# First steps reordered and four weight sums moved to GpSimd, in a one-layer hybrid encoder kernel

## The chip, the cores and the metric

One Trainium2 chip, one core. The metric is device time of the whole kernel in microseconds (us), median over runs. A profile of one execution goes with it: TensorE (PE, with its weight loads PEld), VectorE (DVE), ScalarE (ACT), GpSimd (POOL) and SyncE (SP), which here issues the DMAs.

## The reference

One encoder layer on x, 4096 tokens by 1024 channels, float32. Before everything stands an RMS norm; then one input projection, whose outputs are the attention's q, k, v, a gate g_a, the pooling branch's input u_p and its gate g_p.

```python
h = rmsnorm(x, pre_norm_g[l])
proj = jnp.einsum('bsd,de->bse', h, w_in[l])
q, k, v, g_a, u_p, g_p = jnp.split(proj, splits, axis=-1)
...
a = banded_attention(q, k, v, rel_bias, attn_sink[l]) * jax.nn.silu(g_a)
p = multiscale_pool(u_p, pool_w[l], pool_scale[l]) * jax.nn.silu(g_p)
mixed = jnp.einsum('bse,ed->bsd', jnp.concatenate([a, p], axis=-1), w_out[l])
x = x + rmsnorm(mixed, post_norm_g[l])
```

`rmsnorm` multiplies by the reciprocal root of the mean square and by a gain. Attention looks 128 tokens to each side, with a relative-position bias and a sink logit. `multiscale_pool` takes centred means over 2, 4, 8 and 16 tokens minus the token, maps each channel group by `pool_w` and scales it.

## The kernel before, in words

**Numbers.** A float32 operand is carried as two float16 parts, high and low; a product of two operands is three matmuls (high by high, low by high, high by low). Every operand is first scaled by a power of two that comes from a norm: `scale_pow` and `scale_of` reduce a sum of squares, turn its exponent round with shifts, and write the factor.

**Stages.** A first stage projects the three 512-channel groups called GP (the pooling gate, g_p), GA (the attention gate, g_a) and UU (pooling input times `pool_w`; the kernel multiplies these two weights first, `u_prod`). Tokens come in eight chunks of 512 (m = 0 to 7), each split in halves u = 0, 1 of 256. Each chunk of x has a channel dimension cut in pieces c = 0 to 3 (two 128-channel blocks each). Chunk 0 uses plain 2 by 2 blocks of weights (A11, A12, A21, A22) in `plain`; chunks 1 to 7 use a scheme with fewer products (`quad`) that needs sums of weight blocks, S1 to S4. These sums are made by `sum_weights`: four additions of 128x1024 float32 (`tt`, line 307), each followed by a split into high (`w_high`, ACT, line 606) and low (`w_low`, DVE, line 310). A second stage, with an order written out by hand, makes attention, the output product and the final norm.

**Order.** All of the first stage is given as steps: `do(engine, cost, key, function, reads, writes)`. `Steps.run` is a small planner: at each moment it takes, on the engine that is free first, the ready step with the lowest key, adds the stated cost, and 0.2 for a hand-over to another step. The order so found is the order in which each engine's instructions are issued. So a step's key and stated cost decide its place in the queue of its engine, and an engine that waits at an instruction holds up all that stand behind it. Where a step's key is smaller than that of others that are ready, it goes first; where nothing else is ready, a step far from due is taken.

**The first 30 us.** SP issues the loads by key: the four pieces of x for half 0 (key -9), the gain and an identity matrix, two weight tiles of GP (-8), a small table (-4.5), the other two tiles of GP (-4), x for half 1 (-3.5), two token blocks for the sums of squares of half 1 (-2.3), `pool_w` (9), four tiles `w_uT` for UU (9.5 to 9.8), four tiles of GA (10 to 10.3). PE runs dummy matmuls (`turn_over`) at three places. `first_square` (ACT), `first_add`, `first_fold` (DVE), `first_sum` (PE), `first_eps` (DVE) and `first_root` (POOL) make the reciprocal root of half 0; `spread` (PE) spreads it over the partitions (tile bc). Beside it `gain_most`, `gain_spread` and `gain_scale` make the scale of the gain (tiles gs, gsc, gh). `norm_half` (two instructions on DVE, line 310) multiplies x by gain and root; `b_high` (ACT, line 495) and `b_low` (DVE, line 307) split it. For the weights, `w_square` (ACT), `w_norm` (PE, tiles n2ga for the first two tiles, n2gb for the other two), `w_scale` (DVE), `w_high` and `w_low` give the operands. `row_prod` and `row_keep` are a small product for the attention's bias table. `plain(GP, M0)` then starts the real matmuls (line 689, tile plain), in steps of six matmuls: one block of weights by one piece c.

**Around 64 to 125 us.** DVE prepares chunk 1 (`norm`, `t_sums`, `b_low`, `t_low`), makes S1 to S4 of UU, and starts the pooling of chunk 0 (`pool_tile` on DVE, `pool_gate` on POOL). POOL also makes the reciprocal root of each chunk (`root`). In `quad` the results of UU go into one buffer, ubuf, which the pooling must have left first (a copy, line 908).

Of the kernel before, what the change touches and what calls it, by code (L numbers as in the profile page):

```python
# [8 lines left out]
F32 = mybir.dt.float32  # L9
# [16 lines left out]
NH = 8  # L26
# [108 lines left out]
def hybrid_layer(ctx: ExitStack, tc, io, out):  # L135
# [75 lines left out]
    with ExitStack() as actx:  # L211
# [139 lines left out]
        def row_prod():  # L351
            row_t["p"] = psa.tile([NH, 512], F32, name="fp", tag="n20")
            nc.tensor.matmul(row_t["p"], row_t["b"], row_t["o"], start=True, stop=True)
# [40 lines left out]
        def gain_scale():  # L394
            m2 = comm.tile([P, 1], F32, name="m2", tag="m2")
            V.tensor_reduce(out=m2, in_=bc.pop("g"), axis=mybir.AxisListType.X, op=ALU.max)
            scale_of(gs, m2, 1e-30, H_SCALE)
            t_scalar(V, gsc, g_pre, gs, ALU.mult)
            t_scalar(V, gh, gs, 1.0 / H_SCALE, ALU.mult)
# [10 lines left out]
        do("PE", 2.3, -6, turn_over, 40, r=["ones", "spread0"], w=["bankv"])  # L410
        do("DVE", 1.4, -6, gain_scale, r=["gpre"], w=["gs", "bc"])
# [112 lines left out]
        do("DVE", dve(256), -4, first_fold, w=["xsq3"])  # L524
        do("PE", 0.5, -4, first_sum, r=["onesf", "xsq3"], w=["wup1", "summed"])
        do("DVE", 0.2, -4, first_eps, w=["wup1", "ssq0"])
# [5 lines left out]
        for u in range(2):  # L532
            for i in (2 * u, 2 * u + 1):
                do("PE", 0.3, -3, spread, 0, i, r=["ident", f"rs{u}", "bc"], w=[f"bc{i}"])
            k = (9.4, 19.5)[u]
            for c in range(HK):
                do("DVE", 0.85, k + 0.5 * c, norm_half, c, u,
                   r=["gs"] + [f"bc{i}" for i in (2 * u, 2 * u + 1)],
                   w=[f"n0.{c}.{u}"])
                do("ACT", act(512), k + 0.5 * c + 0.1, b_high, 0, c, u, r=[f"n0.{c}.{u}"],  # L540
                   w=[f"xb0.{c}.{u}h"])
                e, us = ("POOL", 1.4) if c in LOW0[u] else ("DVE", dve(512))
                do(e, us, k + 0.5 * c + 0.2, b_low, 0, c, u,
                   r=[f"n0.{c}.{u}", f"xb0.{c}.{u}h"], w=[f"xb0.{c}.{u}l"])
        for i in range(4):
            w_load(GA, i, 10 + 0.1 * i)
# [35 lines left out]
        def w_scale(group, cols):  # L582
            scale_pow(sw[:, cols], n2_t.pop(group), 1e-20, W_SCALE)
            t_scalar(V, sc[:, cols], sw[:, cols], gh, ALU.mult)
# [5 lines left out]
        def norms(keys, last, views, reads, group, cols):  # L590
# [6 lines left out]
            do("DVE", 1.5, last, w_scale, group, cols, r=["gs"], w=[f"n2{b}", f"sw{group}"])  # L597
# [53 lines left out]
        do("PE", 1.4, 6, turn_over, 24, r=["ones", "swga"], w=["bankv"])  # L651
        do("PE", 0.9, 5.6, row_prod, r=["row", "yt0", "summed"], w=["n20"])
        do("ACT", 0.7, 5.6, row_keep, w=["n20", "yt0"])
        for i, op, key in ((0, A11, 9.5), (1, A12, 12.5)):
# [4 lines left out]
        def gp_gates():  # L659
            w_gates(cg0, slice(0, 4))  # L660
# [10 lines left out]
        do("DVE", 0.2, 20, gp_gates, r=["swga", "swgb"] + [f"xb0.{c}.1l" for c in range(HK)], w=["gates"])  # L671
# [71 lines left out]
        def plain(q, base):  # L743
            ops = {(0, 0): A11, (0, 1): A12, (1, 0): A21, (1, 1): A22}
            for n, (a, h) in enumerate(((0, 0), (1, 0), (0, 1), (1, 1))):
# [3 lines left out]
                for kh in range(2):  # L749
                    for k in range(HK):  # L750
                        op = ops[a, kh]
                        do("PE", 0.66, base + SL * (2 * n + kh) + 0.66 * k, product, bk, tag, q, op,
                           x_b(0, kh, h), kh == 0, kh == 1, range(k, k + 1),
                           r=wkeys(q, op) + [f"xb0.{k}.{h}{v}" for v in "hl"], w=[bkey])
# [231 lines left out]
        sum_weights(UU, sw[:, 8:9], "u4", M1 + 8, 3.0, "DVE")  # L986
# [1206 lines left out]
```

## Time and profile before

| | |
|---|---|
| median of 3 runs | 1162.92 us (1160.59 to 1163.17) |
| profiled execution, own time | 1162.76 us |
| span of the profiled execution | 1161.0 us |
| PE busy | 1146.3 us (99%) |
| DVE busy | 947.8 us (82%) |
| ACT busy | 717.7 us (62%) |
| POOL busy | 313.7 us (27%) |
| mean granted TensorE clock | 0.996 |

A row of the timeline has the start in us, the duration in us, the engine, the line, the operation, the tile written and the tiles read, the shape, how many instructions were merged, and in brackets how long the engine had been idle before and what released it. In the table by windows, each engine's busy us are followed by the number of its instructions, then come the granted clock, the DMA engines' share and GB/s.

### The profile page before, as it was taken

What the parts mean: (1) busy time and instruction counts of PE and PEld (TensorE: products, weight loads), DVE (VectorE), ACT (ScalarE), POOL (GpSimd) and SP (SyncE); (2) the same over time, 40 slices, a digit from 0 to 9 for tenths busy, and PEclk for the clock granted to TensorE, in tenths of its full rate; (3) what the DMA queues carried; (4) which work ended last, traced back from release to release, by engine and by line L of the source; (5) the groups of instructions that cost most, each with busy time, mean ns of one, the idle gap of its engine ahead of it and who ended that gap; (6) DMA issues with size and microseconds to landing.
All of it is one profiled execution on the core that took longest, in us unless ns stands there. A gap on an engine that the chain in (4) does not pass through costs nothing. (4 is left out here: it accounts for less than half of the span.)

```text
span 1161.0 us, 32325 instructions
## 1 busy us (share of the span) xinstructions
PE 1146.3 (99%) x13420; PEld 873.5 (75%) x13420; DVE 947.8 (82%) x1875; ACT 717.7 (62%) x1485; POOL 313.7 (27%) x310
## 2 busy tenths in 40 slices
PE   8999999999999999999999999999999999999997
PEld 7998888888888888886667676576666767667653
DVE  6889988988799974568878888878887888887886
ACT  6876556536654542257676776676667677667772
POOL 0001120211111010201524433532533443353231
PEclk8999999999999999999999999999999999999999
DMA  9645575867667664299975886788777688777885
GB/s 344 217 128 180 174 259 183 285 229 238 227 190 225 206 179 134 76 289 242 250 185 144 197 211 143 200 202 177 177 196 184 148 198 215 140 196 165 178 216 143
DMA packets 301683, 228.36 MB, mean 197 GB/s; under 512 B 219568, under 2 KB 259504, under 8 KB 296928
## 3 DMA queue, kind: packets, MB, share of 16 engines
q1 hardware_dynamic: 301536, 226.30, 72.5%
q8 instruction: 105, 1.72, 0.6%
q14 instruction: 42, 0.34, 0.1%
HBM read 114.68 MB, written 60.34 MB: 151 GB/s over the span
## 5 line engine op out<-in xcount | busy, mean ns | idle before, releaser
L689 PEld LDWEIGHTS <-wq 128*128 128x128 f16 x4104 | 401.6, 98 | 50.4 <-DVE wq L310 2.6
L689 PE MATMUL y<-xt,wq 128*128 128x256 f16 x1512 | 203.3, 273 | 0.1
L1347 ACT ACTIVATE p<-p,nm 128x385 f32<-128x385 f32 (+1 forms) x256 | 152.9, 599 | 36.5 <-POOL p L1330 20.3
L1273 PE MATMUL aq<-xb,xb 128*128 128x256 f16 x1024 | 173.4, 273 | 0.2 <-DVE mo L1715 0.2
L1273 PEld LDWEIGHTS <-xb 128*128 128x128 f16 x1536 | 150.1, 98 | 26.4 <-issue 8.0
L1676 PE MATMUL ms<-wo,ys 128*128 128x512 f16 x720 | 163.7, 379 | 0.0
L1377 DVE SCALAR_TENSOR_TENSOR pn<-p,rd,pn 128x384 f16<-128x384 f32 (+1 forms) x256 | 157.6, 667 | 5.9 <-ACT pn L1369 5.9
L1336 DVE CUSTOM_DVE_ANT_0 p<-s,nt,nsink 128x384 f32<-128x384 f32 (+1 forms) x256 | 156.0, 666 | 2.0 <-PE s L1313 2.0
L1273 PE MATMUL aq<-xb,xt 128*128 128x256 f16 x512 | 139.6, 273 | 0.4 <-issue 0.4
L1369 ACT ACTIVATE pn<-p,rd 128x384 f16<-128x384 f32 (+1 forms) x256 | 134.8, 596 | 4.4 <-issue 1.1
L307 POOL TENSOR_TENSOR yt<-yt,sg 128x512 f32<-128x512 f32 (+2 forms) x32 | 51.0, 1594 | 301.6 <-DVE yt L310 214.8
L1676 PEld LDWEIGHTS <-ys 128*128 128x128 f16 x720 | 68.1, 98 | 83.9 <-POOL ys L1582 4.8
L1676 PE MATMUL m<-wo,y 128*128 128x512 f16 x540 | 121.8, 379 | 0.0
L1676 PEld LDWEIGHTS <-y 128*128 128x128 f16 x540 | 51.4, 98 | 63.5 <-ACT at L1543 2.9
L1273 PE MATMUL kv<-xb,xb 128*128 128x256 f16 x512 | 86.7, 273 | 0.0
L1710 POOL TENSOR_TENSOR mo<-mo,gpost 128x512 f32<-128x512 f32 x39 | 63.7, 1634 | 84.4 <-ACT jkb L1699 83.2
L1273 PEld LDWEIGHTS <-xt 128*128 128x128 f16 x768 | 75.1, 98 | 10.6 <-issue 0.8
L689 PE MATMUL plain<-xb,wq 128*128 128x256 f16 x576 | 68.0, 276 | 2.1 <-DVE wq L310 2.0
L1273 PE MATMUL kv<-xb,xt 128*128 128x256 f16 x256 | 69.8, 273 | 0.0
L689 PE MATMUL v<-xt,wq 128*128 128x256 f16 x504 | 68.6, 273 | 0.1
L689 PE MATMUL v<-xb,wq 128*128 128x256 f16 x504 | 68.6, 273 | 0.0
L689 PE MATMUL y<-xb,wq 128*128 128x256 f16 x504 | 68.6, 273 | 0.0
(221 smaller groups left out, 1854.3 us busy)
## 6 DMA issues: line engine op xcount, KB each, us to landing
nt<-in_xT SPq DMA_DIRECT2D x28, 512.0 KB
x_scr<-xb SPq DMA_DIRECT2D x14, 1024.0 KB
xb<-x_scr SPq DMA_DIRECT2D x14, 1024.0 KB
xr<-in_x SPq DMA_DIRECT2D x28, 512.0 KB
out<-xr SPq DMA_DIRECT2D x28, 512.0 KB
xn<-in_x SPq DMA_DIRECT2D x27, 512.0 KB
ga_scr<-cc SPq DMA_DIRECT2D x64, 128.0 KB
raw<-in_w_out SPq DMA_DIRECT2D x16, 512.0 KB
```

Of the source, the lines that this page charges most:

```text
L307: eng.tensor_tensor(out=out, in0=in0, in1=in1, op=op)
L689: nc.tensor.matmul(b[:, s], wq[:, slot[q, op], wv, s, k, :], x[:, xv, k, :], start=(first and k + s + wv + xv == 0), stop=(last and k == H ...
L1273: nc.tensor.matmul(acc, w[:, j, k, :], x[:, kh, v, kt, :], start=(n == 0), stop=(n == 3 * KT - 1),)
L1336: nc.vector.tensor_tensor_reduce(out=p_t[b, half][:, hh, :nk], in0=s_t[jj][:, gg, :nk], in1=bias[:, h, lo : lo + nk], scale=negc[:, h : h ...
L1347: nc.scalar.activation(p[:, hh, : nk + 1], p[:, hh, : nk + 1], AF.Exp, bias=nm_t[b, half][:, hh : hh + 1], scale=-1.0, accum_out=den_t[b, ...
L1369: nc.scalar.activation(prob_view(b, half)[:, 0, i], p_t[b, half][:, i, :nk], AF.Copy, scale=rd_t[b, half][:, i : i + 1],)
L1377: nc.vector.scalar_tensor_tensor(out=pn4[:, 1, i], in0=p_t[b, half][:, i, :nk], scalar=rd_t[b, half][:, i : i + 1], in1=pn4[:, 0, i], op0= ...
L1676: nc.tensor.matmul(z_t[u, tag], y[:, k, yi, :], wo[o][:, wi, k, :], start=(n == 0 and acc is None), stop=(n == 3 * HK - 1), skip_group_che ...
L1710: eng.tensor_tensor(out=mo, in0=mo, in1=gpost[:, cs], op=ALU.mult)
```

## The change

Five things are edited, all in the first stage.

1. The gain's scale is cut in two: `gain_power` (reduction and `scale_of`, five DVE instructions) gets key -3.9 and must follow `first_fold`; `first_eps` must follow it; `gain_scale` keeps the two multiplications and follows `first_eps`. The second block of dummy matmuls goes from 40 to 28, the third from 24 to 12.
2. `norm_half` of half 0 gets other keys, and for c > 0 must follow a `b_high`; the `w_scale` of GP's first two tiles must follow the first `norm_half`; `w_scale` of GP no longer makes the inverse scales (two DVE instructions each), which `gp_gates` makes once (`w_inverse`). `w_low` and `w_high` of A12 get the key 10.2 (12.5 before).
3. In `plain(GP)` the first group of eight steps takes A11 and A12 in turns: pieces 0 and 1 with A11, pieces 0 and 1 with A12, then piece 2 with both, then piece 3 with both (before: all four pieces with A11, then with A12).
4. The four loads of GA get keys 8.5 to 8.8, ahead of `pool_w` and `w_uT`. `row_prod` must follow the first `w_scale`, in another PSUM tile; `row_keep` gets key 11.5.
5. The four additions of `sum_weights(UU)` go from DVE to POOL.

```diff
-        def gain_scale():
+        def gain_power():
             m2 = comm.tile([P, 1], F32, name="m2", tag="m2")
             V.tensor_reduce(out=m2, in_=bc.pop("g"), axis=mybir.AxisListType.X, op=ALU.max)
             scale_of(gs, m2, 1e-30, H_SCALE)
+
+        def gain_scale():
             t_scalar(V, gsc, g_pre, gs, ALU.mult)
             t_scalar(V, gh, gs, 1.0 / H_SCALE, ALU.mult)
...
-        do("PE", 2.3, -6, turn_over, 40, r=["ones", "spread0"], w=["bankv"])
-        do("DVE", 1.4, -6, gain_scale, r=["gpre"], w=["gs", "bc"])
+        do("PE", 1.6, -6, turn_over, 28, r=["ones", "spread0"], w=["bankv"])
...
+        do("DVE", 0.9, -3.9, gain_power, r=["xsq3"], w=["gs0", "bc"])
         do("PE", 0.5, -4, first_sum, r=["onesf", "xsq3"], w=["wup1", "summed"])
-        do("DVE", 0.2, -4, first_eps, w=["wup1", "ssq0"])
+        do("DVE", 0.2, -3.8, first_eps, r=["gs0"], w=["wup1", "ssq0"])
+        do("DVE", 0.4, -3.7, gain_scale, r=["gpre", "gs0", "ssq0"], w=["gs"])
...
-                do("DVE", 0.85, k + 0.5 * c, norm_half, c, u,
-                   r=["gs"] + [f"bc{i}" for i in (2 * u, 2 * u + 1)],
+                do("DVE", 0.85, k + (0, 0.1, 0.85, 1.5)[c], norm_half, c, u,
+                   r=["gs"] + [f"bc{i}" for i in (2 * u, 2 * u + 1)] + [f"xb0.{min(c - 1, 1)}.0h"] * (u == 0 and c > 0),
                    w=[f"n0.{c}.{u}"])
...
-            w_load(GA, i, 10 + 0.1 * i)
+            w_load(GA, i, 8.5 + 0.1 * i)
...
             scale_pow(sw[:, cols], n2_t.pop(group), 1e-20, W_SCALE)
+            if group not in ("ga", "gb"):
+                w_inverse(cols)
+
+        def w_inverse(cols):
             t_scalar(V, sc[:, cols], sw[:, cols], gh, ALU.mult)
             V.reciprocal(isc[:, cols], sc[:, cols])
...
-            do("DVE", 1.5, last, w_scale, group, cols, r=["gs"], w=[f"n2{b}", f"sw{group}"])
+                us = 1.1 if group in ("ga", "gb") else 1.5
+            do("DVE", us, last, w_scale, group, cols,
+               r=["gs"] + ["n0.0.0"] * (group == "ga"), w=[f"n2{b}", f"sw{group}"])
...
-        do("PE", 1.4, 6, turn_over, 24, r=["ones", "swga"], w=["bankv"])
-        do("PE", 0.9, 5.6, row_prod, r=["row", "yt0", "summed"], w=["n20"])
-        do("ACT", 0.7, 5.6, row_keep, w=["n20", "yt0"])
-        for i, op, key in ((0, A11, 9.5), (1, A12, 12.5)):
+        do("PE", 0.9, 6, row_prod, r=["row", "yt0", "swga"], w=["n21"])
+        do("PE", 0.7, 6.1, turn_over, 12, r=["ones", "swga"], w=["bankv"])
+        do("ACT", 0.7, 11.5, row_keep, w=["n21", "yt0"])
+        for i, op, key in ((0, A11, 9.5), (1, A12, 10.2)):
...
-        do("DVE", 0.2, 20, gp_gates, r=["swga", "swgb"] + [f"xb0.{c}.1l" for c in range(HK)], w=["gates"])
+        do("DVE", 0.6, 20, gp_gates, r=["swga", "swgb"] + [f"xb0.{c}.1l" for c in range(HK)], w=["gates"])
...
-                for kh in range(2):
-                    for k in range(HK):
-                        op = ops[a, kh]
-                        do("PE", 0.66, base + SL * (2 * n + kh) + 0.66 * k, product, bk, tag, q, op,
+                turns = [(kh, k) for kh in range(2) for k in range(HK)]
+                if q == GP and n == 0:
+                    turns = [(kh, k) for ks in ((0, 1), (2,), (3,)) for kh in range(2) for k in ks]
+                for i, (kh, k) in enumerate(turns):
+                    op = ops[a, kh]
+                    do("PE", 0.66, base + SL * 2 * n + 0.66 * i, product, bk, tag, q, op,
...
-        sum_weights(UU, sw[:, 8:9], "u4", M1 + 8, 3.0, "DVE")
+        sum_weights(UU, sw[:, 8:9], "u4", M1 + 8, 3.0, "POOL")
```

More of the change, by code (lines that the diff above doesn't have):

```diff
@@ L351, in row_prod @@
         def row_prod():
-            row_t["p"] = psa.tile([NH, 512], F32, name="fp", tag="n20")
+            row_t["p"] = psa.tile([NH, 512], F32, name="fp", tag="n21")
             nc.tensor.matmul(row_t["p"], row_t["b"], row_t["o"], start=True, stop=True)
@@ L659, in gp_gates @@
         def gp_gates():
+            w_inverse(slice(0, 4))
             w_gates(cg0, slice(0, 4))
@@ L748, in plain @@
                 bk, bkey = f"plain{q}{a}{h}", f"bank{tag}"
-                for kh in range(2):
-                    for k in range(HK):
-                        op = ops[a, kh]
-                        do("PE", 0.66, base + SL * (2 * n + kh) + 0.66 * k, product, bk, tag, q, op,
-                           x_b(0, kh, h), kh == 0, kh == 1, range(k, k + 1),
-                           r=wkeys(q, op) + [f"xb0.{k}.{h}{v}" for v in "hl"], w=[bkey])
+                turns = [(kh, k) for kh in range(2) for k in range(HK)]
[4 more added lines that the diff above has]
+                    do("PE", 0.66, base + SL * 2 * n + 0.66 * i, product, bk, tag, q, op,
+                       x_b(0, kh, h), kh == 0, kh == 1, range(k, k + 1),
+                       r=wkeys(q, op) + [f"xb0.{k}.{h}{v}" for v in "hl"], w=[bkey])
                 t = base + SL * (2 * n + 2) - EV
```

## The prediction

> **What bounds the kernel now.** I read the page first, then PE's own waits in the first 200 us, then a table of windows, and only then the timeline of the first 30 us.
>
> ```profile
> span 1161.0 us, 32325 instructions
> ...
> PE 1146.3 (99%) x13420; PEld 873.5 (75%) x13420; DVE 947.8 (82%) x1875; ACT 717.7 (62%) x1485; POOL 313.7 (27%) x310
> ...
> PE plain L689 <- DVE wq L310: 2.0, 1, 2.0
> ...
> 30.00:40.00 10.00, 10.00 (x109) 9.24 (x108) 9.69 (x27) 9.47 (x15) 0.00 (x0) 1.00 0.99 376
> 40.00:50.00 10.00, 10.00 (x97) 9.28 (x96) 7.42 (x9) 7.70 (x12) 0.00 (x0) 1.00 0.48 165
> 50.00:60.00 10.00, 10.00 (x102) 9.36 (x100) 6.18 (x5) 8.10 (x15) 2.44 (x2) 1.00 0.18 55
> 60.00:70.00 10.00, 10.00 (x98) 9.17 (x97) 7.82 (x16) 9.14 (x12) 0.00 (x0) 1.00 0.34 105
> ...
> 110.00:120.00 10.00, 10.00 (x95) 8.96 (x93) 9.63 (x15) 4.94 (x7) 1.26 (x1) 1.00 0.44 131
> ```
>
> PE is 14.7 us short of the span. The longest of its waits up to 200 us is one of 2.0 us, for the low half of a weight. From 30 to 120 us all nine windows of 10 us show PE busy for 10.00. So only two things in this stretch can shorten the run: real matmuls that begin earlier, and a stall of PE near 125 us (its row is below). An engine that is freed in between is worth what it does for those two places.
>
> The start, from the timeline of all engines:
>
> ```profile
> 7.37 0.28 DVE L396 TENSOR_REDUCE m<-sp 128x1 f32<-128x128 f32 x1
> ...
> 8.44 0.23 DVE L299 TENSOR_SCALAR gsc<-g_pre,gs 128x8 f32<-128x8 f32 x1
> ...
> 8.64 1.14 DVE L307 TENSOR_TENSOR nt<-nt 128x512 f32<-128x512 f32 x2
> ...
> 10.37 0.61 PE L577 MATMUL n2ga<-sq,ones 128*128 128x128 bf16 x8
> ...
> 10.70 1.06 ACT L568 ACTIVATE sq<-wq 128x1024 bf16<-128x1024 f32 x1 [0.84 <-DMA wq<-in_w_a]
> 10.79 0.70 POOL L307 TENSOR_TENSOR rs<-ssq,mhalf 128x2 f32<-128x2 f32 x1 [9.87 <-DVE ssq L299]
> ...
> 11.20 1.01 PE L353 MATMUL fp<-yt,rbias 32*8 32x512 f32 x2 [0.22 <-DMA yt<-in_onehot]
> ...
> 12.14 0.82 PE L443 MATMUL bc<-ident,rs 128*128 128x128 f32 x4
> ...
> 13.00 0.87 DVE L310 SCALAR_TENSOR_TENSOR xb<-xb,gsc,bc 128x256 f32<-128x256 f32 x2 [2.29 <-PE bc L443]
> ...
> 13.85 0.42 DVE L189 TENSOR_REDUCE m<-n2ga 128x1 f32<-128x256 f32 x1
> ...
> 15.08 2.19 ACT L606 ACTIVATE wq<-wq,sw 128x1024 f16<-128x1024 f32 x2 [0.56 <-DVE sw L209]
> ...
> 15.42 0.67 DVE L307 TENSOR_TENSOR xb<-xb,xb 128x512 f16<-128x512 f32 x1
> ...
> 20.76 1.28 DVE L310 SCALAR_TENSOR_TENSOR wq<-wq,sw 128x1024 f16<-128x1024 f32 x1
> ...
> 25.63 2.48 DVE L310 SCALAR_TENSOR_TENSOR wq<-wq,sw 128x1024 f16<-128x1024 f32 x2
> ...
> 26.96 4.37 PEld L689 LDWEIGHTS <-wq 128*128 128x128 f16 x41 [0.37 <-DVE wq L310]
> ```
>
> The last two rows set the first term. PE's weight load waits once more, at 26.96, for the low half of A21, which DVE ends at 25.63 + 1.28 = 26.91. By then PE has done the 48 matmuls of the first group, whatever their order; after it PE does not run dry for 95 us. So the start is worth the difference in when A21's low half is ready, as long as the first group is finished by then.
>
> **The start, worked out.** The gain's seven instructions (7.37 to 8.64) leave the place ahead of the last two additions (1.14), which can then run from about 7.5 to 8.6. The five instructions of `gain_power` (7.37 to 8.44, 1.07) end near 9.7. The root, which ended 1.71 us after these additions before (8.64 + 1.14 = 9.78, and 10.79 + 0.70 = 11.49), needs `first_eps` after `gain_power` and ends near 10.7. That is 0.8 us early, but it is not what `spread` waits for. By the planner's costs, worked by hand for the order alone, the second weight norm now comes ahead of `spread` on PE (before, `row_prod` and `spread` went first). It needs the square of the tile whose load arrives at 10.70: square done 11.76, eight small matmuls (0.61 in the row at 10.37, the last part overlapping what follows: 0.5), then 0.86 from `spread` to `norm_half` (12.14 to 13.00). So `norm_half` begins near 13.15, 0.15 later than before.
>
> From there DVE works without a hole. Up to the scale of the second weight pair it now does four `norm_half` (4 x 0.87), two `w_scale` (2 x 1.2, from 13.85 to ACT's start at 15.08, the inverses having left), three `b_low` (3 x 0.67) and two `w_low` (2 x 1.28): 3.5 + 2.4 + 2.0 + 2.55 = 10.4, to 23.55. The fourth `b_low` hides beside ACT's `w_high` of A21 (2.19 / 2 = 1.10, to 24.65), then `w_low` of A21 takes 1.28: ready at 25.93 against 26.91. **First term: -1.0 us.** It comes from the inverses, the fourth `b_low` and a `norm_half` of half 1, which no longer stand in front of this `w_low`.
>
> The first group has its last two steps free at the fourth `b_low`, 24.2; 12 matmuls and the second `spread` end near 26.0, just in time. Two costs lie under cover: the third block of dummies and `row_prod` (1.01) run while PE waits for `w_low` of A11; without that wait they would cost 1.0 and 0.7. `row_keep` now stands on ACT ahead of the square of the last GP tile: from 15.25, two `w_high` (2.19), `b_high`, `row_keep` and that square (none over 1.06) end by 20.6, and the scale that needs it has its turn on DVE only at 22.3. The wait of the first `w_scale` for `norm_half` queues only `w_high` behind it, and is in the sum.
>
> Whether PE runs at full clock is a matter of windows (granted clock third from the right):
>
> ```profile
> 12.00:16.00 4.00, 4.00 (x35) 3.64 (x35) 2.80 (x10) 3.06 (x4) 0.00 (x0) 0.58 1.06 399
> 16.00:19.00 3.00, 0.99 (x15) 0.76 (x14) 3.00 (x7) 3.00 (x5) 0.00 (x0) 1.00 1.06 403
> 19.00:22.40 3.40, 3.40 (x23) 2.72 (x24) 3.40 (x6) 2.83 (x6) 0.00 (x0) 0.56 1.01 414
> ```
>
> The clock is near half up to 16 us and again from 19 to 22.4, the second time after a stretch with PE busy for 0.99 of 3.00. In the change that stretch holds `row_prod` and two steps of plain, so the slow spell may stay away, or come one spell later. If it lay at 22.4 to 25.8, the 24 matmuls due then (12 from 22.3, 12 more from 24.2; 0.22 each at half clock, 0.11 after) would end near 26.7, and with `spread` the first term would be +0.3. If `spread` is not held behind the weight norm, `norm_half` begins at 10.9 + 0.86 = 11.8 and the term is -2.4. Between these ends I take -1.0, the chain that I can follow row by row. [...]
>
> **The loads of GA.** SP issues them ahead of `pool_w` and `w_uT`, 2.36 MB, which at 399 GB/s (window 12 to 16) is up to 5.9 us; `w_uT` comes up to 5 us later. Its first reader:
>
> ```profile
> 37.83 1.06 PE L938 MATMUL wup<-ws,xt 128*128 128x128 f32 x8
> ```
>
> That is late enough to cover the delay. GA's squares, and after them GA's and UU's weights, can come some 4 us earlier. PE is full there: 0.0 us by itself. What it does is to fill DVE's holes from 40 to 70 us (10 - 7.42, 10 - 6.18, 10 - 7.82: 8.6 us in the windows above), which the next part needs.
>
> **The sums on POOL.** They free DVE of four additions and load POOL, and these two engines get in each other's way:
>
> ```profile
> 98.70 2.17 POOL L307 TENSOR_TENSOR yt<-yt,sg 128x504 f32<-128x504 f32 x1 [4.96 <-DVE yt L310]
> 103.18 1.25 POOL L307 TENSOR_TENSOR yt<-yt,sg 128x504 f32<-128x504 f32 x1 [2.32 <-DVE yt L310]
> ...
> 95.85 1.23 DVE L307 TENSOR_TENSOR xb<-nt,xb 128x1024 f16<-128x1024 f32 x1
> ...
> 99.67 1.76 DVE L307 TENSOR_TENSOR yt<-ubuf 128x527 f32<-128x527 f32 x1
> ...
> 105.44 1.21 DVE L307 TENSOR_TENSOR wq<-wq 128x1024 f32<-128x1024 f32 x1
> ...
> 112.94 0.70 DVE L307 TENSOR_TENSOR ws<-ubuf 128x527 f32<-128x527 f32 x1
> ...
> 124.07 0.74 DVE L310 SCALAR_TENSOR_TENSOR ubuf<-x,uf,cc 128x512 f32<-128x512 f32 x1
> ...
> 101.00 0.82 PE L689 MATMUL y<-xb,wq 128*128 128x256 f16 x6
> ...
> 121.96 0.82 PE L689 MATMUL y<-xt,wq 128*128 128x256 f16 x6
> 122.61 0.82 PE L689 MATMUL v<-xb,wq 128*128 128x256 f16 x6
> 123.55 0.81 PE L689 MATMUL y<-xt,wq 128*128 128x256 f16 x6
> 124.86 0.82 PE L689 MATMUL x<-xb,wq 128*128 128x256 f16 x6 [0.49 <-DVE ubuf L310]
> ```
>
> POOL's multiplication of 504 takes 1.25 by itself (103.18) and 2.17 where DVE was at work; DVE's addition of 527 takes 0.70 by itself (112.94) and 1.76 where POOL was (99.67). Each waits for the other to end. An addition of 1024 on POOL is then 1.25 x 1024 / 504 = 2.5 us (an estimate), four are 10. DVE gets back 4 x 1.21 = 4.8 and loses between 0, if POOL works while DVE has holes, and 10. Net for DVE: from -4.8 to +5.2.
>
> [...]
>
> What PE notices: the last piece of chunk 1 is ready at 95.85 + 1.23 = 97.08 and first used at 101.00, 3.9 us of slack. At the end of the stretch there is none: the step at 123.55 comes 0.94 after the one before it, where steps follow at 0.65, so 0.28 is lost, and 0.49 at 124.86 behind DVE's ubuf. I take it that the additions fall into or near the holes of 40 to 70 us, since UU's weights come earlier and POOL idles, so that DVE is at 95 us no later than before and has less ahead of it up to 125. **Second term: -0.28 - 0.49 = -0.77 us.** Its ends: -0.77, and +5.2.
>
> **The sum.** -1.0 + 0.0 - 0.77 = -1.75, rounded. On the profiled execution, 1162.76 (span 1161.0 and 1.76 around it), this gives 1161.0; the median of the runs shown is 0.16 higher, so 1161.2.
>
> **The rivals.**
> *Slower: DVE is shut out where it is full.* If UU's weights do not come early, POOL adds while DVE is busy for over 9 of 10 us, DVE is 5.2 us late, and PE waits. With 3.9 us of slack at 101.00 PE ends 1.3 us later than before; at the ubuf step, without slack, 5.2. Prices: 1164.2 to 1168.1. It decides once DVE reaches the ubuf step more than 2.3 us after 124.07. For it: the rows at 98.70 and 99.67. Against it: 8.6 us of holes in DVE just ahead. Chance 0.18.
> *Much faster: `spread` is not held by the weight norm.* First term -2.4, sum -3.2: 1159.7. For it: the root is ready at 10.7. Against it: the order by the planner's costs. Chance 0.15.
> *The start gives nothing.* Half clock at 22.4 to 25.8 (+0.3), or one more wait of 1 us on ACT or DVE, with or without the second term: 1162.4 to 1163.2. Chance 0.20.
> Forecast: 0.47, with a range of its own from 1160.2 to 1162.2.
>
> **How the numbers follow.** About 0.2% (2.3 us) is what a measurement of this kernel can tell from no change: below 1160.6 is faster, above 1165.2 slower. Faster: the second rival (0.15) and the lower tail of the forecast (0.07). Slower: most of the first rival (0.16) and a little besides (0.02). The rest, 0.60, is no change. The range from 1159.7 to 1165.2 holds the forecast, the third rival, half of the second and the lower part of the first.
>
> **What would show it.** Right: the first `norm_half` near 13.15, behind the second weight norm on PE; A21's `w_low` ending near 25.9; four POOL additions of 2.5 us or more, before 80 us; DVE fuller from 40 to 70 us; no wait of PE for ubuf. Wrong: waits of PE between 60 and 125 us that were not there, DVE instructions stretched by over 1 us beside POOL's additions, ACT held at the `w_high` of a sum, or `norm_half` starting before 12.5.

## The result, and the profile after

The changed kernel takes 1168.38 us (median of 6, 1167.11 to 1172.6), the kernel before in the same runs 1161.99 (1160.59 to 1163.17, 6): a ratio of 1.0056, 95% interval 1.0044 to 1.0069. It is slower by 6.4 us, where 1161.2 and a range up to 1165.2 were forecast. The profiled execution took 1167.75, 0.6 under its median.

From the page of the changed kernel: the span, the engines, and queue q8 (packets, MB, share of 16 DMA engines), which the counts further down give to PE's code.

```profile
span 1165.7 us, 32249 instructions
...
PE 1143.3 (98%) x13396; PEld 870.1 (75%) x13396; DVE 951.2 (82%) x1869; ACT 718.6 (62%) x1485; POOL 327.3 (28%) x314
...
q8 instruction: 104, 1.70, 0.6%
```

PE does its work in 3.0 us less busy time, and the span is 4.7 longer. Its waits say where (us in total, times, longest):

```profile
PE o L1495 <- DMA pt<-pn: 3.3, 3, 1.3
PE y L699 <- ACT ubuf L785: 3.3, 1, 3.3
...
PE v L699 <- DVE cc L307: 1.3, 1, 1.3
...
PE y L699 <- DVE xb L307: 0.9, 1, 0.9
```

Three of these (for ubuf, cc and xb, all between 96 and 129 us) are new, and the wait for pt, the transposed probabilities of the second stage, has grown; in the kernel before it stood at 1.5 us in two, and its one wait of over 0.15 us between 30 and 500 us was 0.49 for DVE's ubuf. The table by windows, of the projection's matmuls alone (PE busy, then its count in brackets), first before, then after, tells when the time goes:

```profile
0.00:90.00 90.00, 61.12 (x520) 51.04 (x521) 0.96 0.66 225
0.00:200.00 200.00, 169.50 (x1504) 147.29 (x1505) 0.98 0.64 212
0.00:450.00 450.00, 419.19 (x3786) 370.59 (x3787) 0.99 0.67 217
```

```profile
0.00:90.00 90.00, 62.45 (x539) 52.28 (x540) 1.00 0.61 211
0.00:200.00 200.00, 165.97 (x1462) 143.34 (x1463) 0.99 0.62 207
0.00:450.00 450.00, 415.96 (x3747) 366.94 (x3748) 1.00 0.67 213
```

A matmul of this kind takes 0.109 us (a step of six every 0.655). At 90 us the changed kernel is 19 of them ahead (2.1 us), at 200 us 42 behind (4.6 us), and so it stays, 39 behind at 450. The rest of the span's difference comes in the second stage, with the waits for pt.

The start of the changed kernel, from the timeline:

```profile
10.33 1.06 ACT L571 ACTIVATE sq<-wq 128x1024 bf16<-128x1024 f32 x1 [0.59 <-DMA wq<-in_w_a]
11.44 0.61 PE L580 MATMUL n2ga<-sq,ones 128*128 128x128 bf16 x8 [1.04 <-ACT sq L571]
...
11.88 0.66 PE L444 MATMUL bc<-ident,rs 128*128 128x128 f32 x4
...
12.58 0.87 DVE L310 SCALAR_TENSOR_TENSOR xb<-xb,gsc,bc 128x256 f32<-128x256 f32 x2 [2.10 <-PE bc L444]
...
23.41 2.48 DVE L310 SCALAR_TENSOR_TENSOR wq<-wq,sw 128x1024 f16<-128x1024 f32 x2 [0.62 <-ACT wq L615]
```

`spread` (bc) stands behind the second weight norm, as forecast; `norm_half` begins at 12.58, and A21's low half is ready at 23.41 + 1.24 = 24.65.

Where the 2.1 us ahead become 4.6 behind, all engines together:

```profile
76.02 10.88 POOL L307 TENSOR_TENSOR wq<-wq 128x1024 f32<-128x1024 f32 x4 [18.31 <-DVE wq L310]
76.51 2.94 DVE L310 SCALAR_TENSOR_TENSOR wq<-raw,sw,wq 128x1024 f16<-128x1024 f32 x1
79.38 7.81 DVE L307 TENSOR_TENSOR nt<-nt 128x512 f32<-128x512 f32 x3
87.22 1.04 ACT L514 CAST xt<-nt 128x1024 f16<-128x1024 f32 x1 [9.54 <-DVE nt L307]
88.17 0.68 ACT L785 ACTIVATE ubuf<-plain,uf 128x512 f32<-128x512 f32 x1
...
95.52 0.67 ACT L785 ACTIVATE ubuf<-plain,uf 128x512 f32<-128x512 f32 x1
96.24 0.81 PE L699 MATMUL y<-xb,wq 128*128 128x256 f16 x6 [3.33 <-ACT ubuf L785]
```

The same two DVE groups in the kernel before:

```profile
77.43 1.28 DVE L310 SCALAR_TENSOR_TENSOR wq<-wq,com 128x1024 f16<-128x1024 f32 x1
78.62 1.61 DVE L307 TENSOR_TENSOR nt<-nt 128x512 f32<-128x512 f32 x3
```

What released the first addition was DVE's own `w_low` (the row at 76.02 says wq), not a load. The four additions on POOL take 10.88 us, and in that time DVE ends four instructions: 2.94 where 1.28 is usual, 7.81 where 1.61 is. DVE loses (2.94 - 1.28) + (7.81 - 1.61) = 7.9 us. ACT stands 9.54 us at a cast that needs DVE's `t_sums`, and behind that cast in its queue are the evacuations of PSUM into ubuf. The last of them comes at 95.52, and PE, which needs the bank, stands for 3.33.

The windows show what DVE had to spare there (busy us and count of PE, PEld, DVE, ACT, POOL, then the granted clock, the DMA share and GB/s):

```profile
40.00:50.00 10.00, 10.00 (x101) 9.41 (x99) 7.32 (x8) 8.27 (x16) 0.00 (x0) 1.00 0.49 159
50.00:60.00 10.00, 10.00 (x98) 9.29 (x96) 7.53 (x7) 8.97 (x15) 1.90 (x2) 1.00 0.25 80
60.00:70.00 10.00, 10.00 (x98) 9.11 (x96) 7.85 (x17) 7.95 (x10) 0.00 (x0) 1.00 0.24 80
70.00:80.00 10.00, 10.00 (x94) 8.95 (x93) 10.00 (x9) 6.55 (x8) 3.90 (x2) 1.00 0.54 159
80.00:90.00 10.00, 10.00 (x94) 8.96 (x92) 9.93 (x6) 2.78 (x4) 6.74 (x3) 1.00 0.05 9
90.00:100.00 10.00, 6.67 (x49) 5.21 (x48) 9.93 (x13) 7.69 (x11) 1.56 (x2) 0.85 0.67 211
```

The holes from 40 to 70 us are still 7.3 us. The additions ran from 76, where there are none. PE's stall is followed by a granted clock of 0.85 in its window, which is another 1.5 us (0.15 x 10) of full clock.

### The profile page after: what moved, and what is told of

The parts are those of the page before. It is cut to its first block, busy times and chain, and to the rows that moved or that the text cites. A ratio compares the mean times of both kernels' runs of the same rounds, so it can differ in the third digit from the quotient of the medians.

```text
span 1165.7 us, 32249 instructions
## 1 busy us (share of the span) xinstructions
PE 1143.3 (98%) x13396; PEld 870.1 (75%) x13396; DVE 951.2 (82%) x1869; ACT 718.6 (62%) x1485; POOL 327.3 (28%) x314
## 5 line engine op out<-in xcount | busy, mean ns | idle before, releaser
L307 POOL TENSOR_TENSOR yt<-yt,sg 128x512 f32<-128x512 f32 (+2 forms) x32 | 54.2, 1694 | 297.6 <-DVE yt L310 271.6
```

Of the source, the lines that this page charges most:

```text
L307: eng.tensor_tensor(out=out, in0=in0, in1=in1, op=op)
```

## The experiments

Sixteen kernels, in four groups that each shared a chip and the runs of the kernel before (whose medians in the four were 1162.43, 1162.34, 1162.21 and 1162.42). Theory A is the lock: additions on POOL shut DVE out where it is full. The others come as the runs called for them. e3 and e14 leave the sums of UU out and compute the rest.

| run | median us (range, runs) | ratio to before, 95% |
|---|---|---|
| e1_sums_dve | 1165.34 (1162.95 to 1170.36, 11) | 1.0029 (1.0019 to 1.0040) |
| e2_pool_alone | 1169.64 (1168.83 to 1170.91, 4) | 1.0061 (1.0047 to 1.0075) |
| e3_write_only | 1162.14 (1160.08 to 1166.19, 10) | 1.0001 (0.9991 to 1.0012) |
| e4_halves | 1168.04 (1167.31 to 1171.01, 4) | 1.0044 (1.0029 to 1.0060) |
| e5_one_add | 1165.36 (1164.10 to 1167.36, 6) | 1.0025 (1.0014 to 1.0037) |
| e6_ga_back | 1165.74 (1164.73 to 1168.46, 5) | 1.0034 (1.0022 to 1.0046) |
| e7_loads_late | 1166.46 (1163.28 to 1167.36, 5) | 1.0032 (1.0020 to 1.0044) |
| e9_pad48 | 1163.52 (1162.29 to 1168.65, 12) | 1.0015 (1.0004 to 1.0025) |
| e10_after_pad48 | 1168.06 (1167.02 to 1168.94, 4) | 1.0050 (1.0036 to 1.0064) |
| e11_before_less48 | 1165.09 (1163.25 to 1165.76, 8) | 1.0024 (1.0013 to 1.0034) |
| e12_before_plus48 | 1161.95 (1161.04 to 1163.58, 11) | 0.9999 (0.9990 to 1.0008) |
| e13_order_back | 1164.69 (1163.70 to 1166.39, 10) | 1.0023 (1.0014 to 1.0032) |
| e14_write_pad48 | 1160.88 (1159.62 to 1164.94, 11) | 0.9990 (0.9981 to 0.9999) |
| e15_chunks_only | 1162.52 (1161.55 to 1163.20, 11) | 0.9999 (0.9990 to 1.0008) |
| e16_due_early | 1164.43 (1162.31 to 1167.40, 11) | 1.0016 (1.0007 to 1.0025) |
| e17_chunks_plus48 | 1161.64 (1160.68 to 1162.99, 11) | 0.9995 (0.9987 to 1.0004) |

### The additions on POOL

**e1_sums_dve**, all of the change but the move to POOL:

```diff
-        sum_weights(UU, sw[:, 8:9], "u4", M1 + 8, 3.0, "POOL")
+        sum_weights(UU, sw[:, 8:9], "u4", M1 + 8, 3.0, "DVE")
```

> The changed kernel with one thing undone: the four additions of UU's weight sums are back on DVE. Theory A (DVE and POOL shut each other out while POOL adds, DVE falls 8 us behind, ACT stands behind DVE, PE stands behind ACT): the loss goes and the start's gain of about 2 us stays, so 1159.0 to 1161.0, with no wait of PE between 85 and 130 us above 0.5. Theory B (the loss comes from the new order of steps, with sums and their splits standing in other places of ACT's and PE's queues): still slower than before, 1164 or more.

1165.34: the time lies in B's range, the trace has A's sign. Of the three waits between 96 and 129 us those for ubuf and xb are gone and that for cc is down to 0.5, and at 200 us PE has done 1521 projection matmuls, 17 more than before; yet the kernel is still 2.9 us slower than before. So the lock costs some 3.5 us here (6.4 - 2.9), and something else in the new start costs the rest.

**e2_pool_alone**, the kernel before with that one word changed to "POOL" and nothing else.

> The kernel before with this one thing done: the four additions of UU's weight sums on POOL. A: as the changed kernel without its start: 1162 plus some 6.7, 1165.5 to 1170.5, and DVE's instructions beside the additions stretched as in the changed kernel. B: within 1.5 us of the kernel before, 1160.5 to 1163.5.

1169.64, as A said. The additions run at 78.18 for 10.89 us, PE waits 3.3 for ACT's ubuf again, and at 200 us PE is 73 matmuls behind the kernel before (8.0 us). The move alone costs 7.2 us. From 90 to 200 us PE falls back by 61 matmuls against the kernel before, here (12 behind, then 73) as in the changed kernel (19 ahead, then 42 behind): 6.6 us both times. In the new start it costs less net: there, without it, PE waits 1.9 us for DVE further on (at 225, 285 and 330 us), which a PE that is 6 us late does not meet.

**e3_write_only**, fills in place of the additions:

```diff
+            def fill(e, o, x, y, op):
+                for n in range(3):
+                    e.memset(o, 0.01 * (n + 1))
...
-                do(eng, us, k, tt, e, o, x, y, op, r=...
+                do(eng, us, k, fill if eng == "POOL" else tt, e, o, x, y, op, r=...
```

> The changed kernel, but each of the four POOL additions is three fills of the same tile, which read nothing (the weight sums of UU hold constants, so this part of the result is left out). Order of all queues and the waits on POOL's results stay. A: DVE's instructions beside the fills keep their lengths, no wait of PE above 0.5 us between 85 and 130 us, 1158.5 to 1161.0. B: as the changed kernel, 1166 to 1170.

```profile
76.38 11.72 POOL L642 MEMSET wq<- 128x1024 f32 x12 [18.28 <-DVE wq L310]
...
76.90 1.28 DVE L310 SCALAR_TENSOR_TENSOR wq<-raw,sw,wq 128x1024 f16<-128x1024 f32 x1
78.09 1.60 DVE L307 TENSOR_TENSOR nt<-nt 128x512 f32<-128x512 f32 x3
```

POOL is busy on the same tiles for 11.72 us, longer than with the additions, and DVE's two groups take 1.28 and 1.60, as in the kernel before. The median, 1162.14, is 1.1 us above the upper end of A's forecast and 4 below the lower end of B's. So it is neither POOL's being busy on these tiles nor its place in the order that holds up DVE's two groups. The additions, which read two tiles where a fill reads none, do: 7.9 us lost beside 10.88 us of additions, none beside 11.72 us of fills. That it is the reading, and no other difference between an addition and a fill, is the author's inference.

**e4_halves**, each addition on POOL in two of 512:

```diff
+            def halves(e, o, x, y, op):
+                for n in range(2):
+                    tt(e, o[:, n], x[:, n], y[:, n], op)
```

> The changed kernel with each of the four POOL additions cut into two of 128x512. A: POOL holds DVE up for half as long at a time but twice as often; the total for DVE is the same where DVE has more work waiting, so still slower than before: 1164 to 1169. B: no difference to the changed kernel, 1167 to 1170.

1168.04: shorter instructions do not help. Both forecasts hold this time; the trace tells them apart. The eight halves took 14.62 us, and six groups of DVE beside them were stretched by less each (`t_sums` to 4.57 in place of 7.81), by 6.4 us in all.

**e5_one_add**, only the first addition on POOL:

```diff
             add(a22, a21, a22, 2, 3, 3, ALU.add, key - step)
+            eng, e, us = "DVE", V, dve(D)
```

> The changed kernel with only the first of UU's four additions on GpSimd, the other three back on VectorE. Theory A (an addition on GpSimd shuts VectorE out while VectorE is full, and the cost grows with the number of additions): one addition takes about 2.7 us of GpSimd and costs VectorE some 2 us instead of 7.9, so the time lies between that with none (1165.3) and that with four (1168.4): 1165.3 to 1166.8, with no wait of PE for ACT's ubuf in 80 to 110 us. Rival B (the loss is one of order, not of the amount: any move to GpSimd makes it): 1167.5 or more.

1165.36, A's lower end. One DVE group is stretched, to 2.94 us, so DVE loses 1.7 us and not 7.9. At 200 us PE stands 15 matmuls behind e1 (1506 to 1521), but 7 of them it was behind at 70 us, before the addition began; the other 8 are 0.9 us. The full change is 6 ahead of e1 at 70 us and 59 behind at 200, 7.1 us. So the loss grows with the number of additions, and the first is less than a quarter of it. It does not show in the median.

### The other 2.9 us, and PE's code fetches

In e1's trace the loss sits in the second stage, whose order is written out by hand and is the same in every kernel. Three rows:

```profile
538.69 0.25 PE L1495 MATMUL o<-pt,vv 128*64 128x128 f16 x2 [2.81 <-DMA pt<-pn]
...
1113.34 0.25 PE L1495 MATMUL o<-pt,vv 128*64 128x128 f16 x2 [1.62 <-DMA pt<-pn]
...
1134.38 0.25 PE L1495 MATMUL o<-pt,vv 128*64 128x128 f16 x2 [0.66 <-DMA pt<-pn]
```

The kernel before waits 0.78 for the first and nothing for the other two. The transposes of pn to pt behind the first two are issued 6.4 and 8.5 us ahead of PE's need in both kernels; they land later. Behind the first wait the granted clock falls too, which it does not in e9 below (e1, then e9):

```profile
540.00:550.00 10.00, 10.00 (x109) 6.45 (x106) 8.29 (x20) 3.34 (x7) 2.52 (x3) 0.84 1.11 198
```

```profile
540.00:550.00 10.00, 10.00 (x116) 6.80 (x115) 8.45 (x21) 6.11 (x16) 2.52 (x3) 1.00 1.16 185
```

That is another 1.6 us of full clock lost in e1's profiled execution, which took 1166.73, 1.4 over its median. Among the packets of the DMA engines in the last microseconds before these waits is one of q8, here of the window 1132 to 1133:

```profile
q1 hardware_dynamic: 132, 0.22, 94.1%
q8 instruction: 1, 0.02, 6.0%
```

q8 moves 105 packets and 1.72 MB in the kernel before, which has 2 x 13420 PE instructions: divided out, 64 bytes for each, and 256 to a packet of 16 KB. In all traces PE starts about 255 instructions from one packet to the next (the medians are 250 to 258; 253 in the kernel before, 256 in the changed one). The profile calls q8 "instruction" and names no engine; from these counts it is taken for PE's own code, and the place of a fetch then depends on how many PE instructions lie ahead of it. The new start has 24 dummy matmuls fewer (28 and 12 in place of 40 and 24), 48 instructions with their weight loads. Over the 18 kernels' profiled executions, 53 of PE's 58 waits for pt have a q8 packet that began 2 to 4.5 us before PE went on, where by chance some 27% would (70 packets in 650 us, one in 9.3). The converse does not hold: PE takes up pt behind a semaphore 1728 times in them; 438 times with such a packet, of which 53 waited, and 1290 times without, of which 5 did. So a packet there goes with nearly every wait, and most such packets go with none. Theory F is that the fetch makes the transpose late; it was tested by padding.

**e9_pad48**, e1 with the 48 instructions put back in a gap in which PE waits:

```diff
-        do("PE", 5.5, -9, turn_over, 52, r=["ones"], w=["bankv", "turned"])
+        do("PE", 5.5, -9, turn_over, 76, r=["ones"], w=["bankv", "turned"])
```

> The new start with UU's sums on VectorE, and the first turn_over with 76 idle matmuls instead of 52: 24 matmuls with their weight loads, 48 PE instructions, put into a gap of 1.96 us in which PE waits for VectorE at 5.5 us. Nothing else changes, the order of all other work included. PE has as many instructions ahead of the second stage as in the kernel before. Theory F: the code fetches fall where they fell before, PE's waits for pt after 1100 us (2.3 us) go, that at 538 us falls from 2.8 to about 0.8, and the time is 1161.5 to 1163.5. Theories G and L (loads in another order, or ahead of the transposes): no change, 1164.5 to 1166.5, or a little more if the idle matmuls delay the start.

1163.52, at the upper end of F: 1.2 us over before, where e1 is 2.9 over. No wait for pt of over 0.3 is left after 600 us, and that at 537 us is 0.54:

```profile
PE o L1495 <- DMA pt<-pn: 1.3, 2, 0.8
PE x L699 <- DVE ubuf L310: 1.2, 1, 1.2
PE v L699 <- DVE cc L307: 1.2, 3, 0.5
...
PE o L1525 <- DMA pt<-pn: 0.5, 2, 0.3
```

Twenty-four matmuls that compute nothing made e1 faster, by 1.7 us of its 2.9; the other 1.2 stay. The clock is a rival here, for e1's executions have a median granted clock of 0.995 and the kernel before 0.998. But at 0.995 to 0.996 alone the medians are 1165.34 for e1 (7 executions), 1163.5 for e9 (4) and 1162.96 for the kernel before (13).

**e11_before_less48**, the reverse, in the kernel before:

```diff
-        do("PE", 2.3, -6, turn_over, 40, r=["ones", "spread0"], w=["bankv"])
+        do("PE", 2.3, -6, turn_over, 16, r=["ones", "spread0"], w=["bankv"])
```

> The kernel before, with 16 idle matmuls instead of 40 in the second turn_over: 48 PE instructions fewer, nothing else changed, the work and its order those of before. Theory F: its code fetches now fall where those of the new start fall, PE waits 1 us or more for pt at two places after 1100 us, where it waited for none, and the time rises by 1 to 2.5 us to between 1163.4 and 1165. If F is wrong: 1161.3 to 1162.9, no wait for pt after 1100 us (or a shift of the start alone, if the idle matmuls held the clock up).

1165.09, 2.9 us slower than before and 0.1 over F's range, with the order of all work unchanged. The two late waits are there:

```profile
1109.12 0.25 PE L1483 MATMUL o<-pt,vv 128*64 128x128 f16 x2 [0.89 <-DMA pt<-pn]
...
1130.93 0.25 PE L1483 MATMUL o<-pt,vv 128*64 128x128 f16 x2 [1.12 <-DMA pt<-pn]
```

At 450 us of this execution PE has done 3783 projection matmuls, 3 fewer than before, so its start is not it. But it took 1163.25, the fastest of the eight, and its waits for pt after 480 us are only 1.5 us more than before (3.2 to 1.7). In the others the clock had a part: the median granted clock is 0.995, and 0.998 in the kernel before. At 0.995 to 0.996 alone e11 has a median of 1165.05 (5 executions), 2.1 us over the kernel before at that clock. The rest of the 2.9 us goes with the clock; whether the idle matmuls that are missing lowered it was not tried.

**e12_before_plus48**, 48 instructions more in the kernel before (third turn_over, 24 to 48).

> The kernel before, with 48 idle matmuls instead of 24 in the third turn_over, which runs in a gap of 2.01 us in which PE waits for VectorE's wq: 48 PE instructions more. Theory F: the code fetches come 48 instructions sooner than in the kernel before; the fetches that stood 2.5 and 4 us ahead of its waits for pt at 536 and 574 us (0.78 and 0.68 us) come 1 to 2 us sooner and miss those transposes, and none comes near the two after 1100 us: 1160.5 to 1162. If F is wrong: 1162 to 1163.5.

The trace did what F said: the waits at 536 and 574 us are gone, and one of 0.26 is the longest left for pt. The median, 1161.95, lies 0.26 under before and inside F's range, but its interval holds 1: what the trace saves does not show in the times.

**e10_after_pad48**, the changed kernel with the padding of e9.

> The changed kernel as it is, UU's sums on GpSimd, with 76 idle matmuls instead of 52 in the first turn_over (48 PE instructions more, as many as the kernel before has ahead of its second stage). Theory F (code fetches of PE that meet a transpose): PE's two waits for pt after 1100 us (2.0 us) go, and the time falls by 1 to 2.5 us, from 1168.4 to between 1165.9 and 1167.4; the loss to GpSimd's additions stays. If F is wrong: 1167.9 to 1169.5.

1168.06: outside F's range by 0.7 us, and in the range given for F being wrong. Of the two late waits one is gone and the other is 0.56, but the fall is not to be told from none. The two spans (1165.7 and 1165.5) agree with that: PE's wait for xb at the end (0.6), which stands in the kernel before too, is back. So the 48 instructions are not worth a fixed sum; in the changed kernel they are worth little. All waits for pt fell by 2.1 us (3.3 to 1.2) and the span by 0.2; what took up the rest of the difference is not shown.

Two rivals for the same loss:

**e6_ga_back**, e1 with GA's loads due at 10 again (`w_load(GA, i, 10 + 0.1 * i)`).

> The new start with UU's sums on VectorE, and GA's loads back at their old due time (10 in place of 8.5). Without this edit it takes 1165.3, 2.9 us over the kernel before. Theory G (GA's loads ahead of pooled's reorder the first stage, and that is the 2.9 us): 1161.5 to 1163.5. Theory F (the new start has 48 PE instructions fewer, so PE's code fetches of 16 KB come at other points of the second stage, and meet the transposes of pn to pt): the count of instructions is unchanged here, so 1164 to 1167, and PE again waits 1 us or more for pt after 1100 us.

1165.74, and 2.1 us of waits for pt after 1100 us: G falls. At 90 us PE stands at 535 matmuls, as in e1 (534), so the loads ahead of `pool_w` are worth nothing there. At 200 us it is 12 behind e1 (1509 to 1521, 1.3 us), after a wait of 1.9 us for cc at 124 us that is 0.5 in e1; in the medians (1165.74 and 1165.34) that is not told apart.

**e7_loads_late**, e1 with the large loads put behind the transposes:

```diff
-    at_(36.5, load_x, U - 3)
+    at_(44.0, load_x, U - 3)
...
-    at_(0.5, load_xr, 1, 1)
-    at_(0.6, load_xr, 1, 0)
+    at_(10.35, load_xr, 1, 1)
+    at_(10.36, load_xr, 1, 0)
```

> The new start with UU's sums on VectorE, and in the second stage the loads that are issued just ahead of two late transposes put behind them: load_x of pair U-3 from 36.5 to 44, both load_xr of pair 1 from 0.5 to 10.35. Theory L (these loads, 1 MB each, hold the DMA engines while the transposes wait): PE's waits for pt at about 538 and 1113 us go, and 1161.5 to 1163.5. Theory F (PE's code fetches hit the transposes): the fetches stay where they are, the waits stay within 1 us of the 5.1 us of before this edit, and 1164 to 1167.

1166.46, with 4.8 us of waits for pt in place of 5.1. Of the two waits that L named, one fell from 2.8 to 0.8 and the other is gone, but 2.65 came up at 576 us and 1.3 at 1134 us in their place. By the time and by the sum of the waits L falls; that the loads shift which transposes are late stays possible.

### What became of the lead

**e13_order_back**, e9 without the order of chunks in the first unit of `plain` and what goes with it.

> The new start with UU's sums on VectorE and the 48 instructions put back (1163.5), and with the first unit of plain in its old order of chunks, norm_half's due times and chain undone, A12 back at 12.5. Theory C (the order of the token chunks and of norm_half is what gave PE its lead): the 527 to 539 projection matmuls that stand at 90 us with the new start fall to 525 or fewer, 520 being the count of before. Rival S (the lead comes from the square sums and gain being ahead, and the shorter turn_over): 527 or more. The first stage is ordered anew behind it, so the total may move by 1 to 2 us either way: 1162.5 to 1165.5.

517 at 90 us: C, and the whole lead goes with this part. **e15_chunks_only** is the other way round, this part alone in the kernel before:

```diff
-                for kh in range(2):
-                    for k in range(HK):
+                turns = [(kh, k) for kh in range(2) for k in range(HK)]
+                if q == GP and n == 0:
+                    turns = [(kh, k) for ks in ((0, 1), (2,), (3,)) for kh in range(2) for k in ks]
```

> The kernel before with one part of the change alone: the first unit of plain takes the chunks of tokens in turn against two weight tiles, norm_half's due times and chain go with it, and A12 is due at 10.2 instead of 12.5. Count of PE instructions, square sums, gain, loads and sums as before. Theory C: this part is the lead, 528 or more projection matmuls at 90 us instead of 520; the fetches fall where they fell before. With C and the lead kept: 1160.5 to 1161.7. With the lead lost between 200 and 350 us, as with the new start as a whole: 1161.8 to 1163.

519 at 90 us (526 in e17 below, whose start is the same and whose granted clock was 1.00 in the first 40 us): C as put here falls. The chunk order is needed for the lead, but does not make it alone; which other part of the start it needs was not tried. The time is that of before.

**e14_write_pad48**, e3 with the padding of e9.

> The changed kernel with UU's sums left out (GpSimd fills in their place, which read nothing) and 76 idle matmuls instead of 52 in the first turn_over. Theory D (PE's lead from the new start, 7 to 19 projection matmuls or 0.8 to 2.1 us, reaches the end once VectorE has room and the code fetches miss the transposes): 1159.7 to 1161.2, at 450 us still 10 or more matmuls ahead of the 3786 of before. Theory H (a lead in the first stage is given back whatever VectorE has to do): 1161.7 to 1163.

1160.88, ratio 0.9990 (0.9981 to 0.9999): D by the time, though the profiled execution had a low clock at its start and stood only 4 matmuls ahead at 450 us, not 10. With UU's sums left out (4.8 us of DVE) the new start is 1.5 us faster than the kernel before; with them on DVE (e9) it is 1.2 us slower. The kernel before without the sums was not run, so part of the 1.5 may be the work that is left out. The clearer pair is e1 and e3, without padding: at 200 us both have their lead (1521 and 1523 matmuls, 1504 before), and at 450 us e3 is 22 ahead of the kernel before and e1 3 behind.

**e16_due_early**, e9 with the planner's due times moved (`M0, SL = 17.0, 2.65`).

> The new start with UU's sums on VectorE and the 48 PE instructions put back (1163.5), and M0, from which the due times of all of the first stage behind the start are counted, at 17 instead of 19. Theory O (the lead is lost because the planner's order for VectorE no longer fits PE that runs ahead of the due times: norm steps stand ahead of the fold into ubuf that PE waits for at 285 us): with the due times moved by the lead, PE's waits for VectorE in 200 to 350 us fall from 2.4 us to under 1, and 1160.5 to 1162.3. Theory D2 (VectorE simply has no room there): the waits stay over 1.5 us, 1163 to 1164.5.

1164.43. In 200 to 350 us PE's waits for DVE were 1.9 us in e9 (the 2.4 counts one at 123 us as well), and here they are 0.2: O's mark in the trace is met. The time did not fall, and it lies in D2's range, though D2's mark (waits over 1.5) is not met. The profiled execution was the slowest of the eleven (1167.40). In it PE was late before it came there: at 200 us it had done 1495 matmuls, 19 fewer than e9, and at 350 us both had done 2861. So the earlier due times moved the loss and did not remove it; whether DVE lacks room or only order stays open. What can be seen is the place, in e1 (PE, then DVE):

```profile
285.15 1.47 PE L699 MATMUL x<-xb,wq 128*128 128x256 f16 x12 [1.22 <-DVE ubuf L310]
```

```profile
281.69 1.61 DVE L307 TENSOR_TENSOR nt<-nt 128x512 f32<-128x512 f32 x3
283.22 1.22 DVE L307 TENSOR_TENSOR xb<-nt,xb 128x1024 f16<-128x1024 f32 x1
284.35 0.74 DVE L310 SCALAR_TENSOR_TENSOR ubuf<-x,uf,cc 128x512 f32<-128x512 f32 x1
```

The planner, which saw no wait here, put the next chunk's `t_sums` and `b_low` ahead of the fold into ubuf that PE needs.

**e17_chunks_plus48**, e15 with the 48 instructions of e12.

> The chunk order alone in the kernel before, and 48 idle matmuls instead of 24 in the third turn_over. Theory F: as in the kernel before with these 48 instructions more, PE's waits for pt at 536 and 574 us go and none comes after 1100 us. 0.2 to 1 us under the same kernel without the 48: 1159.8 to 1161.5 with the lead kept. If the third turn_over no longer lies in a wait, because the chunk order has shortened it: 0.5 to 1.3 us over it.

1161.64, 0.9 under e15, and the waits at 536 and 574 us are gone, though one of 0.3 came at 1108 us, where F had none; against the kernel before it is not told apart (0.9987 to 1.0004). No version that computes everything beats the kernel before by more than its interval.

## Why the prediction was wrong, by its steps

**The first term (-1.0 us) held in its mechanism and was too small.** `spread` did wait for the second weight norm. But that tile's square began at 10.33, not 10.70, so `norm_half` began at 12.58 and not at 13.15, and A21's low half was ready at 24.65 in place of 25.93. By the prediction's own measure that is 2.3 us ahead of the 26.91 of before. By matmuls done at 90 us, eleven profiled executions with the new start have 518 to 539 (mean 530.5), four with the old one 508 to 520 (mean 515.8): 14.7 x 0.109 = 1.6 us. The spread within each is in part the clock granted in the first 40 us, which was 0.91 in the execution shown of before and 1.00 in that of after. The term lay between its ends, -2.4 and +0.3. The second end supposed half clock from 22.4 to 25.8 us; the changed kernel's trace shows a granted clock of 1.00 there, and of 1.00 in the whole of the first 40 us. That the term would reach the end of the run was taken for granted, since PE does not run dry after it. That failed: in e1 the 17 matmuls ahead at 200 us are 3 behind at 350, given back in the waits at 225, 285 and 330 us, and e9 has the same waits.

**The loads of GA were worth 0.0 at 90 us**, as said (e6), and perhaps 1.3 us at 200, which no median shows. What was said to follow did not: UU's weights did not come 4 us earlier. The last `norm` and `w_low` ahead of the additions moved by about 1 us, and the holes of 40 to 70 us stayed (7.3 us left; 8.6 before).

**The second term (-0.77 us) is the step that failed**: "I take it that the additions fall into or near the holes of 40 to 70 us". They began at 76.02, 11.9 us behind the end of the last hole (0.35 us, up to 64.13), in a window with DVE at 10.00 of 10, and they waited for a `w_low` that DVE itself did in that window. The choice between the ends -4.8 and +5.2 for DVE was made on that. DVE lost 7.9 us beside POOL and was relieved of 4.8 us of additions, which had stood later in its queue than the place where it lost them. In place of -0.77 us PE lost 6.6 us from 90 to 200 us.

**The slower rival was the case that came, and it was priced too low.** It had the mechanism (DVE shut out where full) and 1164.2 to 1168.1, with a chance of 0.18; the change took 1168.38. An addition on POOL took 2.72 us where 2.5 was estimated, which is little. What its price left out is the way to PE: it was looked for at DVE's piece of chunk 1, with 3.9 us of slack, but the loss went through ACT's queue, where the evacuations stood behind a cast that waited for DVE. It also left out the clock after the stall, 0.85 in its window. The move alone came to 7.2 us (e2), more than DVE's net of 7.9 - 4.8. That the rival's upper end lies 0.3 us under the measured time is in part luck: its 5.2 us were for DVE alone, and the measured 6.4 holds other losses as well.

**What was not there at all: the number of PE instructions.** The shorter `turn_over` was costed only by whether dummies lie in a wait. The 48 instructions cost 1.7 us between e1 and e9 and 2.9 us between the kernel before and e11, part of that with a lower clock. That they do so by moving every later code fetch, and some of them onto a transpose, is argued from the traces. In the changed kernel itself the padding brought back 0.5 us (6.4 over before, 5.9 in e10), within the intervals, so its share there is not settled.

Together: of the 6.4 us the lock is 3.5 (against e1), or 4.7 with both padded (5.9 in e10, 1.2 in e9), and the rest goes with the number of PE instructions and a lead that the first stage gives back; how it splits between these is not settled.

## What to carry to other kernels

Before an operation goes to an engine whose work stretches that of the engine it leaves, as POOL's additions did here (DVE's 1.28 and 1.61 us to 2.94 and 7.81), find when its inputs are ready and look at the busy time of the engine it leaves in exactly that window. Here it was full, so 7.9 of the additions' 10.88 us were lost there, and ACT (9.54 us) and PE (3.33 us), which stood behind, paid for it. A lead at the start is worth something only if every engine that feeds PE later has room for it; e3 against e1 is the same lead with and without 4.8 us of DVE work. When variants differ by a few tenths of a per cent, keep the count of instructions ahead of the sensitive stage the same, or test each with dummies put in and taken out.

## What the hardware showed that was not expected

- What by its counts is PE's code (q8) stands among the DMA packets of the data: 105 packets of 16 KB in the kernel before, a median of 253 PE instructions apart, one in about 9 us in the second stage. Of 58 waits of PE for a DMA transpose (0.15 to 2.8 us) 53 had such a packet 2 to 4.5 us before, but only 53 of 438 uses with one waited. Removing 24 dummy matmuls cost 2.9 us (e11), adding 24 saved 1.7 (e9). That the fetch makes the transpose late is argued from this, not shown packet by packet.
- Two stalls of PE were paid twice: behind waits of 3.33 us (changed kernel) and 2.81 us (e1) the granted clock was 0.85 and 0.84 in a window of 10 us. Around e11's late waits of 0.89 and 1.12 us it stayed 1.00.
- POOL's fills on SBUF (11.72 us) left DVE's instructions at their usual 1.28 and 1.60 us, while POOL's additions stretched them to 2.94 and 7.81.
